# The recurrence's gate projection as seven products, with tokens on partitions

## The chip, the cores and the metric

The kernel runs on one core of a Trainium2 chip. Its time is the device time of one execution in microseconds (us). It uses five engines: TensorE (PE) multiplies matrices, VectorE (DVE) and ScalarE (ACT) work elementwise, GpSimd (POOL) does a little arithmetic and issues slow transfers, SyncE (SP) issues most loads. Each engine runs its own list of instructions in order, and a semaphore makes it wait where it needs another engine's result or a transfer.

## What is computed

One layer on x, 512 tokens by 2048 features, in float32:

```python
h = rms_norm(x, norm_w)
q, k, v, g_attn, xr, g_lru = split(h @ w_in)      # w_in: 2048 x (1024|256|256|1024|1024|1024)
attn_out = attention(q, k, v)                     # 8 heads, 2 key/value heads, q and k normed and roped
lru_out = rg_lru(xr, forward) + rg_lru(xr, backward)
mixed = concat(rms_norm(attn_out) * silu(g_attn), rms_norm(lru_out) * silu(g_lru))
return x + mixed @ w_out                          # w_out: 2048 x 2048
```

The change concerns g_lru, the 1024 columns of w_in that start at C_GL = 3584.

## The kernel before

**Precision.** A float32 operand is held as a pair of rounded tiles, high and low part: x as xh and xl, a weight tile as wh and wl. mm3 makes one product out of three matmuls: high by high, high by low, low by high. A weight tile of 128 x 512 is loaded by SP into wr (three buffers of two tiles), ACT rounds it to wh (wsplit, L219), DVE subtracts to get wl (L221). x is normed by norm_w alone; the factor 1/rms of a token, rstd, is multiplied in when a projection leaves PSUM.

**Two layouts.** proj_feat gives features on partitions and tokens along the row (the weight tile is the stationary operand): four PSUM banks of 128 features x 512 tokens. Its result has to be multiplied by rstd along the row, so rows() turns rstd (128 x 4) by a transpose on PE, copies the line to line_sb on DVE, writes it to DRAM and reads it back broadcast to all partitions as rbc (two transfers on POOL's queue, L295 and L296). evac_bc then multiplies a bank by rbc on DVE (L395) into an ev tile and so frees the bank. proj_tok gives tokens on partitions; evac_tok scales by rstd[:, t] on ACT. PSUM has eight banks: four for projections (pj) and four for the rest (mm).

**Stages.** PE's instructions run in the order of the program, which weaves a projection (fill) with a chain that consumes earlier results: weave() takes from the chain how many units of fill to run next. The stages are:
- C_XR, first half, while x is still being loaded and split; then xstats makes rstd and rbc.
- C_XR + 512 woven with the recurrence of the first half (lru_half(0)); C_K (k and v) with the second (lru_half(1)).
- C_Q and C_Q + 512 woven with kv(). Each q half ends in evac_tok and norm_rope: ACT sums squares (L533), POOL makes the factors (L281, L282), DVE multiplies and ropes (L538 to L547). kv() also makes r_l, the factor 1/rms of the recurrence's output, and its broadcast gbc.
- gates(): C_GL, C_GL + 512 and the first half of C_GA, 96 units of six to twelve matmuls, woven with attention(). attention() first turns q of two heads (turned(): four transposes each, split by ACT L562 and DVE L563 into the pair b), yields 13 units, and then asks for the first scores. In between normed() multiplies hp, the recurrence's output, by gbc, and gate() multiplies by the silu of the gates.
- C_GA + 512 woven with later(), and then the output projection. It is already done as seven products of half size instead of eight (Strassen's scheme in Winograd's form), whose sums of w_out are made in DRAM by transfers that accumulate: sums_in_dram() issues 32 of them on POOL's queue, one for every second unit of gates().

DVE, ACT and SP get their order from a scheduler that sorts by priority and by when operands come. Weight splits stand under high_priority(AHEAD = 600), the attention's softmax under a smaller one. The order of PE and, in the attention's part, of POOL is that of the code.

**Ring.** aring and hring are rings of SBUF from which the late tiles are cut; hp holds the recurrence's output by feature, ap_ the attention's (av).

Of the kernel before, what the change touches and what calls it, by code (L numbers as in the profile page):

```python
# [17 lines left out]
P = 128  # L18
# [13 lines left out]


LRU_K2, LRU_B4 = 12, 9
ATT_K2, ATT_B4, ATT_PT = 9, 4, 2


AHEAD = 600
# [6 lines left out]


SOON = 40


H = 256  # L50
# [9 lines left out]
def hybrid_kernel(  # L60
# [68 lines left out]

    def ev():  # L130

        for pool, n in (("lru", 4), ("qkv", 8), ("fin", 4)):
            if pool in pools:
                return pools[pool].tile([P, SEQ], F32, tag="ev", bufs=n, name=nm("ev"))

# [9 lines left out]
    def f(ap):  # L145
        return ap.bitcast(F32)
# [11 lines left out]
    nhalf = const([P, 48], "nhalf")  # L158
    nc.gpsimd.memset(nhalf, -0.5)

    nw_st = const([KT, P], "nw_st")
    vec_st = const([R_END, P], "vec_st")

    def vec_load():
# [139 lines left out]

    def proj_feat(c0, acc, first=None, given={}):

        acc += [pj() for _ in range(4)]
        for c in range(KT // 2):  # L310
            if c == 0 and first:

                for k, (wh, wl) in enumerate(first):
                    for j, (w, x_) in enumerate(((wh, xh), (wl, xh), (wh, xl))):
                        for e in range(4):
                            nc.tensor.matmul(  # L316
                                acc[e], w[:, e * P : (e + 1) * P], x_[k],
                                start=k == 0 and j == 0, stop=False,
                            )
# [5 lines left out]
            ws = given[c] if c in given else wload(w_in, c * 2 * P, c0)  # L325
            for e in range(4):
                es = slice(e * P, (e + 1) * P)
                for k, (wh, wl) in enumerate(ws):
                    kk = 2 * c + k
                    mm3(acc[e], wh[:, es], wl[:, es], xh[kk], xl[kk], kk == 0, kk == KT - 1)  # L330
                yield c, e

    def tok_block(acc, w, r0, c0, lh, ll, nk):

        acc += [pj() for _ in range(NT)]
        for c in range(nk // 2):
            ws = wload(w, r0 + c * 2 * P, c0)
            for t in range(NT):
# [222 lines left out]
    def split_ps(pt, hi, lo):  # L561
        nc.scalar.copy(hi, pt)  # L562
        nc.vector.tensor_sub(lo, pt, f(hi))  # L563

    def kv(es):
# [15 lines left out]
        r = group_rstd(sums["l"], "r_l", NB * P)  # L581
        yield 4
        rows(gbc, r)

    def turned(rot, h):

# [36 lines left out]
    def values(h, pth, ptl):  # L623

        gs = slice(h // G * HD, (h // G + 1) * HD)
        o = mm()
        for s in range(NT):
            mm3(o, vh[s][:, gs], vl[s][:, gs], pth[:, s, :], ptl[:, s, :], s == 0, s == NT - 1)
        if h % 2 == 0:
            ap_[h // 2] = aring.tile([P, 2, SEQ], F32, name=nm("av"))  # L630
        av, asum = ap_[h // 2][:, h % 2, :], sums["a"]
        nc.vector.tensor_copy(av, o)
        if h == 0:
            nc.scalar.activation(asum, av, AF.Square)
        else:
            sq = k2()
            nc.scalar.activation(sq, av, AF.Square)
            nc.gpsimd.tensor_add(asum, asum, sq)

    def attention(rots):  # L640

        qs, ps_, pts = {h: turned(rots[0], h) for h in range(2)}, {}, {}
        yield 13
        for d in range(2 * NH + 3):
            h, half = divmod(d - 4, 2)
            if h >= 0 and half == 0:
# [128 lines left out]
        for c in range(4)  # L775
    ]

    def sums_in_dram():

        def two(c, k, j):  # L780
            r0 = mixed[2 * c][0]
            w = w_out[r0 : r0 + 4 * P, j * SEQ : (j + 1) * SEQ]
            return w.rearrange("(n k p) e -> p k n e", k=2, p=P)[:, k]

        def put(c, t, src):
            nc.gpsimd.dma_start(tsum[c][t], src)

        def add(c, t, src):
            nc.gpsimd.dma_start(tsum[c][t], src, accum_op=ALU.add)

        for c0 in (0, 2):
            cs = (c0, c0 + 1)
# [4 lines left out]
                yield add(c, TA, two(c, 0, 0))  # L797
                yield add(c, TB, two(c, 0, 0))
            for c in cs:
                yield put(c, TC, tsum[c][TA])  # L800
            for c in cs:
                yield add(c, TC, two(c, 1, 0))
            for c in cs:
                yield put(c, TD, tsum[c][TC])
            for c in cs:
                yield add(c, TD, two(c, 1, 1))

    def out_loads(g, second, i):

# [226 lines left out]

    s1.close()
    lru_consts()
    jobs = sums_in_dram()
    fill = proj_feat(C_XR + SEQ, a2)  # L1040
    weave(fill, lru_half(0, a1))
    drain(fill)
# [20 lines left out]

    def both():
        yield from q_proj(C_Q, a4)
        yield from q_proj(C_Q + SEQ, a5)

    fill = both()
    weave(fill, kv(kvs))
    drain(fill)  # L1070

    closed("rot", "rope", "wx")
    sums["a"] = pools["qkv"].tile([P, SEQ], F32, tag="asum", name="asum")
    opened("att", "right")

    late = []

    def gates():
        todo = iter(())
        for n, (c0, row) in enumerate(((C_GL, R_LN), (C_GL + SEQ, R_LN + 4), (C_GA, R_AN))):  # L1080
            acc, wait = [], 8 * (n > 0)
            for k, _ in enumerate(proj_feat(c0, acc)):
                if 32 * n + k >= 16 and k % 2 == 0:
                    next(jobs, None)
                if n == 0 and k >= 16 and k % 4 == 0:
                    normed(hp[k // 4 - 4])
                if wait == 0:
                    wait = next(todo, 99)
                wait -= 1
                yield  # L1090
            if n < 2:
                todo = gate(evac_bc(acc), hp[2 * n : 2 * n + 2], row, k2)
            else:
                late.extend(evac_bc(acc))

    fill = gates()
    with tc.manual_schedule(engines={mybir.EngineType.Pool}):
        weave(fill, attention(rots))
        for _ in range(6):
            next(fill)  # L1100
    r = group_rstd([sums["a"]], "r_a", NH * HD)
    closed("att", "qkv")
# [17 lines left out]
    def later():  # L1120
        for pair in ap_[:2]:
            normed(pair)
        yield 6
        todo = gate(late, ap_[:2], R_AN, fin_s)
        for _ in range(3):
            yield next(todo)
# [82 lines left out]
```

## Time and profile before

| | us |
|---|---|
| median of 3 runs | 650.33 (650.0 to 650.38) |
| the profiled execution, own time | 650.22 |
| its span | 648.4 |
| PE busy | 643.5 (99%) |
| DVE busy | 476.4 (73%) |
| ACT busy | 347.1 (54%) |
| POOL busy | 94.8 (15%) |

The span is the time from the first to the last instruction in the trace; about 1.8 us of the execution lie around it. PE's busy time counts overlapping matmuls once. The gates run from 255 to about 440 us, the output projection after it.

### The profile page before, as it was taken

The numbers are of one execution on the slowest core, as the hardware profiler recorded it, in microseconds if no ns is written. First come the engines' busy times: TensorE is split into PE (matmuls) and PEld (weight loads), VectorE is DVE, ScalarE is ACT, GpSimd is POOL, SyncE is SP. The second block draws the span as 40 slices with busy tenths as digits, with TensorE's granted clock in tenths as the row PEclk, the third lists the DMA queues.
The fourth block names the chain that finished last, engine by engine and source line by source line (L and its number), as shares of the span: only waits on it lengthen the run. The fifth ranks groups of instructions, "written<-read, shape, count | busy, mean of one in ns | idle before, by whom it ended". The sixth has DMA issues, their size and how long they took to land.

```text
span 648.4 us, 8619 instructions
## 1 busy us (share of the span) xinstructions
PE 643.5 (99%) x2979; PEld 534.0 (82%) x2979; DVE 476.4 (73%) x821; ACT 347.1 (54%) x639; POOL 94.8 (15%) x126
## 2 busy tenths in 40 slices
PE   9999999999999999999999999999999999999997
PEld 6888888888888888888888888888888888888886
DVE  5877679986788935855765566637967978699994
ACT  3543799489856615444474444635444654443441
POOL 0000000000012312123434435311000000010000
PEclk9999999999999999999999999999999999999999
DMA  8943243322234331357676858763354857686322
GB/s 290 304 128 111 66 137 99 92 71 66 83 99 144 98 114 33 109 148 173 117 191 174 204 122 202 184 131 113 98 184 166 324 166 238 202 281 211 120 92 98
DMA packets 53211, 96.96 MB, mean 150 GB/s; under 512 B 4332, under 2 KB 14960, under 8 KB 53040
## 3 DMA queue, kind: packets, MB, share of 16 engines
q1 hardware_dynamic: 45936, 75.56, 36.6%
q0 software_dynamic: 7056, 20.72, 14.2%
q8 instruction: 23, 0.38, 0.2%
q14 instruction: 20, 0.16, 0.1%
q10 hardware_dynamic: 176, 0.14, 0.1%
HBM read 92.21 MB, written 20.98 MB: 175 GB/s over the span
## 4 chain that ended last, share of the span: by engine, by line
PE 99%; DVE 0%; issue 0%
PE pj L150 20%; PE pj L151 20%; PE pj L149 20%; PE mm L944 13%; PE pj L944 11%; PE mm L151 3%; PE mm L149 3%; PE mm L150 3%; PE mm L619 2%; PE mm L251 1%; PE pj L316 1%; PE mm L558 1%; PE mm L983 0%; PE mm L692 0%; DVE xt L927 0%; PE mm L292 0%
## 5 line engine op out<-in xcount | busy, mean ns | idle before, releaser
L149 PE MATMUL pj<-x,wh 128*128 128x512 f32 x376 | 147.6, 392 | 0.0
L151 PE MATMUL pj<-x,wl 128*128 128x512 f32 x376 | 146.5, 390 | 0.0
L150 PE MATMUL pj<-x,wh 128*128 128x512 f32 x376 | 146.5, 390 | 0.0
L219 ACT CAST wh<-wr 128x512 fp32r<-128x512 f32 x143 | 85.0, 619 | 76.4 <-PE pj L151 18.7
L221 DVE TENSOR_TENSOR wl<-wr,wh 128x512 fp32r<-128x512 f32 (+1 forms) x145 | 101.1, 724 | 33.3 <-ACT wh L219 32.7
L150 PEld LDWEIGHTS pj<-x,wh 128*128 128x128 f32 x376 | 70.6, 188 | 14.9 <-DVE x L254 0.4
L151 PEld LDWEIGHTS pj<-x,wl 128*128 128x128 f32 x376 | 70.6, 188 | 14.8
L149 PEld LDWEIGHTS pj<-x,wh 128*128 128x128 f32 x376 | 70.6, 188 | 14.7
L755 ACT CAST oh<-rw 128x512 fp32r<-128x512 f32 x94 | 56.3, 620 | 38.7 <-PE mm L944 15.5
L149 PE MATMUL pj<-wh,x 128*128 128x512 f32 x192 | 75.0, 391 | 0.0
L151 PE MATMUL pj<-wh,x 128*128 128x512 f32 x192 | 74.7, 389 | 0.0
L150 PE MATMUL pj<-wl,x 128*128 128x512 f32 x192 | 74.7, 389 | 0.0
L756 DVE TENSOR_TENSOR ol<-rw,oh 128x512 fp32r<-128x512 f32 x94 | 61.9, 688 | 10.7 <-ACT oh L755 10.4
L944 PE MATMUL mm<-ol,mh 128*128 128x512 f32 (+1 forms) x128 | 49.0, 382 | 0.0
L944 PE MATMUL mm<-oh,ml 128*128 128x512 f32 (+1 forms) x128 | 48.9, 382 | 0.0
L944 PE MATMUL mm<-oh,mh 128*128 128x512 f32 (+1 forms) x128 | 48.9, 382 | 0.0
L149 PEld LDWEIGHTS pj<-wh,x 128*128 128x128 f32 x192 | 36.0, 188 | 7.6
L150 PEld LDWEIGHTS pj<-wl,x 128*128 128x128 f32 x192 | 36.1, 188 | 7.4
L151 PEld LDWEIGHTS pj<-wh,x 128*128 128x128 f32 x192 | 36.0, 188 | 7.4
L944 PE MATMUL pj<-oh,mh 128*128 128x512 f32 (+1 forms) x104 | 39.7, 382 | 0.0
L944 PE MATMUL pj<-ol,mh 128*128 128x512 f32 (+1 forms) x104 | 39.7, 382 | 0.0
L944 PE MATMUL pj<-oh,ml 128*128 128x512 f32 (+1 forms) x104 | 39.6, 381 | 0.0
(209 smaller groups left out, 1062.9 us busy)
## 6 DMA issues: line engine op xcount, KB each, us to landing
wr<-in_w_in_dram SPq DMA_DIRECT2D x71, 512.0 KB, 3.8
rw<-in_w_out_dram SPq DMA_DIRECT2D x63, 256.0 KB, 3.8
ts<-in_w_out_dram POOLq DMA_DIRECT2D x24, 512.0 KB, 6.6
rw<-ts SPq DMA_DIRECT2D x31, 256.0 KB, 4.4
ts<-ts POOLq DMA_DIRECT2D x8, 512.0 KB, 8.0
xt<-in_x_dram SPq DMA_DIRECT2D x8, 512.0 KB, 8.6
b<-in_x_dram SPq DMA_DIRECT2D x7, 512.0 KB, 7.8
out_dram<-xt POOLq DMA_DIRECT2D x12, 256.0 KB, 3.4
```

Of the source, the lines that this page charges most:

```text
L149: nc.tensor.matmul(acc, lh, rh, start=start, stop=False)
L150: nc.tensor.matmul(acc, lh, rl, start=False, stop=False)
L151: nc.tensor.matmul(acc, ll, rh, start=False, stop=stop)
L219: rounded(hi[:, c], raw[:, k, c])
L221: nc.vector.tensor_sub(lo[:, c], raw[:, k, c], f(hi[:, c]))
L251: nc.tensor.transpose(pt[:, t * P : (t + 1) * P], xc[:, h * n + t, ks], ident)
L316: nc.tensor.matmul(acc[e], w[:, e * P : (e + 1) * P], x_[k], start=k == 0 and j == 0, stop=False,)
L558: nc.tensor.transpose(pt[:, t * P : (t + 1) * P], rot[t][:, h, :], ident)
L619: nc.tensor.transpose(pt[:, s * P : (s + 1) * P], p[:, s * P : (s + 1) * P], ident)
L755: nc.scalar.copy(hi, src)
L756: nc.vector.tensor_sub(lo, src, f(hi))
L944: nc.tensor.matmul(bank[key][:, to], lh[:, a, ts_], rh[:, cols], start=i == 0 and j == 0, stop=i == 7 and j == 2,)
```

## The change

It makes C_GL's projection in seven products, each of 256 tokens x 512 columns x 1024 features, on two PSUM banks (gl_units). The products are named P1, Q6, P2, Q5, Q3, Q7, Q4.
- **Weight sums.** Four combinations of w_in's blocks for each of four chunks (gsum) are made in DRAM by 32 accumulating transfers on POOL's queue, by the same sums_in_dram as for w_out. These and w_out's now form one list, jobs["all"]. paced() takes one from the list with each weight load from C_XR + 512 on (two at every fifth): DVE copies one column of the newest wl to a mark, POOL copies the mark, and then POOL issues the transfer. gates() takes one from it for every third unit.
- **Sums of x.** x_sums(i), for i = 0 to 7, makes z = xh + xl for two tiles (DVE, 128 x 512 each), then d, four combinations of 128 x 256 (three DVE subtractions, the first 128 x 512), and POOL stores d (512 KB) in DRAM as dsum (ds in the rows below). d and z have two buffers each. Two of the eight run before C_XR + 512 in the program, six during the second q half. In four of the products they come back as draw, 16 loads of 256 KB, and are split into dh (ACT) and dl (DVE).
- **Combining.** product_done adds or subtracts a product's two banks into ev tiles (14 on DVE, 2 copies on ACT); 10 ev tiles instead of 8.
- **Gates.** They come out with tokens on partitions. lru_gates(j) applies silu with scale rstd and the factor r_l by ACT, turns the tiles back by 8 groups of four transposes on PE, and multiplies into hp on DVE. hp's multiplication by gbc, and r_l's rows(), go.
- **C_GA's first half** runs as two passes of 256 columns (ga_units, G and H) among C_GL's units, in the order of PLAN; the heads 0 and 1 are gated early (heads_gates).
- **Attention** yields 4 units ahead of its first scores instead of 13; av is copied on ACT instead of DVE; the pools k2 and b4 are smaller.

```diff
+    def x_sums(i):
+        z, d = zs[i % 2], ds_[i % 2]
+        for k in range(2):
+            nc.vector.tensor_add(z[:, k, :], f(xh[2 * i + k]), f(xl[2 * i + k]))
+        src, a = halves(z), nc.vector.tensor_tensor
+        a(d[:, 0:2], src[:, 0:1].broadcast_to([P, 2, H]), src[:, 1:3], op=ALU.subtract)
+        a(d[:, 2], src[:, 1], d[:, 1], op=ALU.subtract)
+        a(d[:, 3], src[:, 3], d[:, 2], op=ALU.subtract)
+        nc.gpsimd.dma_start(dsum[i // 2][:, :, i % 2, :], d)
...
     def attention(rots):
         qs, ps_, pts = {h: turned(rots[0], h) for h in range(2)}, {}, {}
-        yield 13
+        yield 4
...
             elif d < 2 * NH + 2:
-                yield sum(STEPS)
+                yield 2
...
+    for i in range(XS_FIRST):
+        x_sums(i)
+    jobs["all"] = itertools.chain(sums_in_dram(gsum, two_gl), sums_in_dram(tsum, two_out))
     fill = proj_feat(C_XR + SEQ, a2)
     weave(fill, lru_half(0, a1))
...
+        for n, _ in enumerate(q_proj(C_Q + SEQ, a5)):
+            if n % 4 == 3 and n // 4 + XS_FIRST < KT // 2:
+                x_sums(n // 4 + XS_FIRST)
+            yield
...
+    def gl_units(banks):
+        nd = 0
+        for name, left, right in PRODUCTS:
+            for c in range(4):
+                with tc.high_priority(AHEAD):
+                    raw = pools["wr"].tile([P, 2, SEQ], F32, tag="wr", bufs=3, name=nm("wr"))
+                    nc.sync.dma_start(
+                        raw, gsum[c][right] if isinstance(right, int) else two_gl(c, *right)
+                    )
+                    if isinstance(left, int):
+                        draw = draws[nd % 2]
...
+                        nc.scalar.copy(dh, draw)
+                        nc.vector.tensor_sub(dl, draw, f(dh))
+                    ws = [wsplit(raw, n) for n in range(2)]
+                for n, (wh, wl) in enumerate(ws):
+                    i = 2 * c + n
+                    for s, bank in enumerate(banks):
...
+                        mm3(bank, lh, ll, wh, wl, i == 0, i == KT // 2 - 1)
+                    if i == KT // 2 - 1:
+                        product_done(name, banks)
+                    yield name if i == KT // 2 - 1 else None
...
+    def lru_gates(j):
+        tiles = [halves_of[n, s] for n in (("c", "d"), ("b", "a"))[j] for s in range(2)]
+        for t, tile_ in enumerate(tiles):
+            nc.scalar.activation(tile_, tile_, AF.Silu, scale=rstd[:, t : t + 1])
+        yield
+        for t, tile_ in enumerate(tiles):
+            nc.scalar.activation(tile_, tile_, AF.Identity, scale=r_lru[0][:, t : t + 1])
+        yield
+        for m in range(4):
+            pt = mm()
+            for t, tile_ in enumerate(tiles):
+                nc.tensor.transpose(
+                    pt[:, t * P : (t + 1) * P], tile_[:, m * P : (m + 1) * P], ident
+                )
...
+    PLAN = "uuuuG" "uuuuG" "uuuuG" "uuGuuG" "uuGuuG" "uuuuG" "uuuu" "HHHHHHHH"
```

The order moves at two seams. The first is the end of C_XR's first half. POOL's list there, before, has rstd, then the line and the broadcast rbc, and then the factors of k:

```order
L281 TENSOR_SCALAR rstd<-xsum 128x4
L282 TENSOR_TENSOR rstd<-rstd,nhalf 128x4
L295 DMA line_601<-line_sb 4x128
L296 DMA rbc<-line_601 128x512
L281 TENSOR_SCALAR rr_1683<-rr_1683 128x2
```

Now, with ds the stores of d_719 and d_720 (the two buffers of d), L285 and L286 the former L281 and L282, and L299 and L300 the former L295 and L296:

```order
L848 DMA ds_141<-d_719 512x1x256
L285 TENSOR_SCALAR rstd<-xsum 128x4
L286 TENSOR_TENSOR rstd<-rstd,nhalf 128x4
L848 DMA ds_141<-d_720 512x1x256
L299 DMA line_629<-line_sb 4x128
L300 DMA rbc<-line_629 128x512
L321 COPY mark_91<-mark_91 128x1
L817 DMA gs_125<-in_w_in_dram 256x1x512
```

One store stands ahead of rstd and one between rstd and the line. DVE's list up to line_sb's copy at the same place, before, holds the constants of the recurrence (lc):

```order
L371 RECIPROCAL lc_659<-lc_659 128x16
L372 TENSOR_TENSOR lc_659<-lc_659,lc_658 128x16
L373 TENSOR_TENSOR lc_660<-lc_659 128x16
L374 TENSOR_SCALAR lc_661<-lc_660 128x16
L376 TENSOR_TENSOR lc_661<-lc_661,lc_660 128x16
L377 TENSOR_SCALAR lc_661<-lc_661 128x16
L293 COPY line_sb<-mm_598 4x128
```

Now L843 is a sum z, and L845, L846 and L847 are the three subtractions of d:

```order
L225 TENSOR_TENSOR wl_653<-wr_650,wh_652 128x512
L225 TENSOR_TENSOR wl_657<-wr_650,wh_656 128x512
L189 COPY vec<-mm_591 128x104
L845 TENSOR_TENSOR d_720<-z_718 128x512
L386 TENSOR_SCALAR lc_685<-vec 128x16
L843 TENSOR_TENSOR z_717<-x_92_385,x_93_386 128x512
L387 TENSOR_TENSOR lc_685<-lc_685,vec 128x16
L846 TENSOR_TENSOR d_720<-z_718,d_720 128x256
L297 COPY line_sb<-mm_626 4x128
```

The copy to line_sb stands behind the subtraction that writes d_720 anew, which needs the store of d_720 to have ended.

The second seam is the start of the gates. PE's list ahead of the first scores, before (b_509 is the pair of head 0's q, kt_2208 the keys; pj_2522 to pj_2525 are the banks of C_GL, thirteen units after the transposes of q):

```order
L150 MATMUL pj_2522<-x_62_313,wh_2630 128x512
L151 MATMUL pj_2522<-x_61_312,wl_2631 128x512
L149 MATMUL pj_2522<-x_64_321,wh_2634 128x512
L150 MATMUL pj_2522<-x_65_322,wh_2634 128x512
L151 MATMUL pj_2522<-x_64_321,wl_2635 128x512
L149 MATMUL mm_2644<-kt_2208,b_509_2506 128x512
L150 MATMUL mm_2644<-kt_2208,b_509_2506 128x512
L151 MATMUL mm_2644<-kt_2208,b_509_2506 128x512
```

Now (b_533_2705 is the same pair, and pj_2721 and pj_2722 are the first product's banks, four units after the transposes):

```order
L152 MATMUL pj_2721<-wh_2754,x_82_340 128x512
L153 MATMUL pj_2721<-wl_2755,x_82_340 128x512
L154 MATMUL pj_2721<-wh_2754,x_83_341 128x512
L152 MATMUL pj_2722<-wh_2754,x_82_340 128x512
L153 MATMUL pj_2722<-wl_2755,x_82_340 128x512
L154 MATMUL pj_2722<-wh_2754,x_83_341 128x512
L152 MATMUL mm_2771<-kt_2365,b_533_2705 128x512
L153 MATMUL mm_2771<-kt_2365,b_533_2705 128x512
L154 MATMUL mm_2771<-kt_2365,b_533_2705 128x512
```

There are 24 matmuls between the transposes and the scores instead of 78. DVE's list there, before, ends the rope work of the second q half (sq_2491 and ev_2427 are its last tile) and then splits q of heads 0 and 1 (L563):

```order
L538 TENSOR_TENSOR ev_2427<-ev_2427,rr_2462 128x512
L540 TENSOR_TENSOR sq_2491<-ev_2427,rq 128x8x32 x2
L546 TENSOR_TENSOR ev_2427<-ev_2427,rq 128x512
L547 TENSOR_TENSOR ev_2427<-ev_2427,sq_2491 128x512
L221 TENSOR_TENSOR wl_2631<-wr_2628,wh_2630 128x512
L563 TENSOR_TENSOR b_509_2506<-mm_2507,b_509_2506 128x512
L221 TENSOR_TENSOR wl_2635<-wr_2628,wh_2634 128x512
L563 TENSOR_TENSOR b_511_2514<-mm_2515,b_511_2514 128x512
```

Now, with L582 the split of q, dl the low parts of the reloaded sums of x, and mx the first row maximum of the scores:

```order
L557 TENSOR_TENSOR ev_2623<-ev_2623,rr_2658 128x512
L565 TENSOR_TENSOR ev_2621<-ev_2621,rq 128x512
L559 TENSOR_TENSOR sq_2687<-ev_2623,rq 128x8x32
L566 TENSOR_TENSOR ev_2621<-ev_2621,sq_2681 128x512
L559 TENSOR_TENSOR sq_2687<-ev_2623,rq 128x8x32
L565 TENSOR_TENSOR ev_2623<-ev_2623,rq 128x512
L566 TENSOR_TENSOR ev_2623<-ev_2623,sq_2687 128x512
L1180 TENSOR_TENSOR dl_2895<-draw_2701,dh_2894 128x512
L1180 TENSOR_TENSOR dl_2949<-draw_2702,dh_2948 128x512
L582 TENSOR_TENSOR b_533_2705<-mm_2706,b_533_2705 128x512
L582 TENSOR_TENSOR b_535_2713<-mm_2714,b_535_2713 128x512
L626 TENSOR_REDUCE mx_2775<-mm_2771 128x1
```

The split of q stands behind all of the rope work still, and behind two low parts that were not there before.

More of the change, by code (lines that the diff above doesn't have):

```diff
@@ L303, in xstats, with paced @@
         rows(rbc, rstd)
+    jobs, job_of = {}, [0]
+    def paced(ws):
+        if "all" in jobs:
+            wl = ws[1][1]
+            for _ in range(2 if job_of[0] % 5 == 3 else 1):
+                m = marks[job_of[0] % len(marks)]
+                job_of[0] += 1
+                nc.vector.tensor_copy(m[:, 0:1], f(wl[:, 0:1]))
+                nc.gpsimd.tensor_copy(m[:, 8:9], m[:, 0:1])
+                next(jobs["all"], None)
     def proj_feat(c0, acc, first=None, given={}):
@@ L580, in kv @@
             split_ps(turn(rot, h), kth[h], ktl[h])
-        r = group_rstd(sums["l"], "r_l", NB * P)
-        yield 4
-        rows(gbc, r)
+        r_lru.append(group_rstd(sums["l"], "r_l", NB * P))
     def turned(rot, h):
@@ L1079, in gates @@
         todo = iter(())
[L1080 to L1092, printed above, removed]
-            else:
-                late.extend(evac_bc(acc))
+        for n, unit in enumerate(itertools.chain.from_iterable((u, u) for u in PLAN)):
+            done = next(units[unit])
+            if n % 3 == 0:
+                next(jobs["all"], None)
+            if done == "Q4":
+                todo = itertools.chain(todo, lru_gates(1))
+            elif unit == "G" and len(early) == 2 and n == PLAN.rindex("G") * 2 + 1:
+                todo = itertools.chain(lru_gates(0), heads_gates(early))
+            else:
+                next(todo, None)
+            yield
@@ L1123, in later @@
         yield 6
-        todo = gate(late, ap_[:2], R_AN, fin_s)
-        for _ in range(3):
-            yield next(todo)
+        todo = gate(late, ap_[1:2], R_AN + 2, fin_s)
+        yield next(todo)
         drain(
```

130 lines of the change are left out of this document (113 added, 17 removed).

## The prediction

> **What bounds the kernel now.** I read first the busy time and the waits, then the chain that ended last. These rows are the page's line of busy times, its row of the granted TensorE clock, the one row of the view of waits that belongs to PE, and the head of the chain.
>
> ```profile
> PE 643.5 (99%) x2979; PEld 534.0 (82%) x2979; DVE 476.4 (73%) x821; ACT 347.1 (54%) x639; POOL 94.8 (15%) x126
> PEclk9999999999999999999999999999999999999999
> PE mm L983 <- DVE ones L156: 1.0, 1, 1.0
> PE 99%; DVE 0%; issue 0%
> ```
>
> PE works 643.5 of 648.4 us, the chain is PE from end to end, and PE's only wait on another engine in the whole run is 1.0 us at the very start. So two questions decide: how much PE work the change removes, and whether PE, which never waits today, begins to wait. Every microsecond of either goes into the end whole. DVE (73%) and ACT (54%) matter only where PE comes to wait for them. Next I read the timeline of PE, for the price of a matmul and of a group of transposes.
>
> ```profile
> 53.72 0.39 PE L150 MATMUL pj<-x,wh 128*128 128x512 f32 x1
> ...
> 56.89 0.39 PE L149 MATMUL pj<-x,wh 128*128 128x512 f32 x1
> ...
> 58.48 0.39 PE L150 MATMUL pj<-x,wh 128*128 128x512 f32 x1
> ...
> 296.02 0.60 PE L558 MATMUL mm<-ident,ev 128*128 128x128 f32 x4
> 296.37 0.48 PE L149 MATMUL mm<-kt,b 128*128 128x512 f32 x1
> 296.69 0.40 PE L150 MATMUL mm<-kt,b 128*128 128x512 f32 x1
> ```
>
> A record lasts 0.39 us, but the records overlap. From 53.72 to 58.48 lie 21 steps, so a matmul costs 4.76/21 = 0.2267 us. Four transposes hold the next matmul off by 0.35 (296.02 to 296.37), and that matmul is followed after 0.32 instead of 0.23, so a group of four costs about 0.44.
>
> **The matmuls.** C_GL's 1024 columns took 2 x 16 x 4 x 3 = 384 matmuls; seven products of 8 k-tiles x 2 banks x 3 are 336. Removed: 48 x 0.2267 = 10.9 us. The gates now come out with tokens on partitions, and 8 groups of four transposes turn them: 8 x 0.44 = 3.5. One transposed row fewer (r_l) is below my rounding. C_GA's first half in two passes of 256 columns keeps its count. PE's own work falls by 7.4 us.
>
> **Start of C_XR+512 (first seam).** The four banks of C_XR are freed by evac_bc, which multiplies by rbc, the broadcast of rstd. These are the steps to rbc in the timelines of DVE and POOL, in order of time, and below them DVE's load in two stretches.
>
> ```profile
> 43.21 0.19 DVE L300 TENSOR_REDUCE xsum<-ssq 128x4 f32<-128x32 f32 x1
> 43.49 0.56 POOL L281 TENSOR_SCALAR rstd<-xsum 128x4 f32<-128x4 f32 x1 [42.17 <-DVE xsum L300]
> 44.13 1.04 POOL L282 TENSOR_TENSOR rstd<-rstd,nhalf 128x4 f32<-128x4 f32 x1
> 49.12 0.27 DVE L293 COPY line_sb<-mm 4x128 f32<-4x128 f32 x1
> 51.80 0.60 POOL L296 DMA_DIRECT2D rbc<-line  x1 [1.35 <-DMA line<-line_sb]
> 55.64 1.89 DVE L395 TENSOR_TENSOR ev<-pj,rbc 128x512 f32<-128x512 f32 x3 [2.18 <-DMA rbc<-line]
> 20.00:40.00 20.00, 20.00 (x108) 16.95 (x107) 16.43 (x52) 10.40 (x18) 0.00 (x0) 1.00 0.80 269
> 40.00:60.00 20.00, 20.00 (x90) 16.39 (x90) 15.25 (x53) 5.37 (x10) 2.92 (x4) 1.00 0.40 119
> ```
>
> line_sb to the first eviction takes 6.5 us, the bank is free at 55.64 + 1.89/3 = 56.3, and PE takes it at 56.89: slack 0.6. In the new order three things come ahead. DVE gets some twenty x_sums operations (0.69 us each) among C_XR's, where it is already busy 16.43 and 15.25 of 20 us; by a walk along its rows xsum comes near 45.4 instead of 43.2, and rstd near 47.4. Then POOL issues the transfer ds of the second d right after rstd, and on DVE line_sb's copy now stands behind the subtraction that overwrites that d, so behind the landing. No 512 KB store like it is in this trace. The nearest rows of the DMA issues:
>
> ```profile
> out_dram<-xt POOLq DMA_DIRECT2D x12, 256.0 KB, 3.4
> ts<-in_w_out_dram POOLq DMA_DIRECT2D x24, 512.0 KB, 6.6
> ts<-ts POOLq DMA_DIRECT2D x8, 512.0 KB, 8.0
> ```
>
> The first has the direction with half the bytes, the second the bytes; I take 5, with 3.4 and 8.0 as ends. After landing, the waiting subtraction, one sum, one half-wide subtraction and two small constants run ahead of the copy, about 2.2 us: 47.4 + 5 + 2.2 = 54.6. Six and a half later, plus 0.7 for the eviction, gives 61.8 for the bank, against a demand of 57.5 (0.6 later than before, since one z stands ahead of an early xl on whose heels PE runs). Stall 4.3, and with that 0.6: **+4.9**, ends 3.3 and 7.9. If the scheduler's sums were covered after all it would be 0. The lc constants and wh casts behind line_sb have their cover in the same wait.
>
> **Start of the gates and of attention (second seam).** The last q chunk ends, eight transposes turn q of heads 0 and 1, and attention yields 13 gate units before its first scores; now it yields 4. The timelines of PE, ACT and DVE there, and the load of the engines:
>
> ```profile
> 254.56 0.39 PE L151 MATMUL pj<-wh,x 128*128 128x512 f32 x1
> 254.78 1.03 PE L558 MATMUL mm<-ident,ev 128*128 128x128 f32 x8
> 255.57 0.48 PE L149 MATMUL pj<-x,wh 128*128 128x512 f32 x1
> ...
> 273.36 0.39 PE L149 MATMUL mm<-kt,b 128*128 128x512 f32 x1
> ...
> 266.37 0.58 ACT L562 CAST b<-mm 128x512 fp32r<-128x512 f32 x1
> ...
> 255.26 0.69 DVE L538 TENSOR_TENSOR ev<-ev,rr 128x512 f32<-128x512 f32 x1 [5.05 <-POOL rr L282]
> ...
> 267.76 0.69 DVE L547 TENSOR_TENSOR ev<-ev,sq 128x512 f32<-128x512 f32 x1
> 268.37 0.68 DVE L221 TENSOR_TENSOR wl<-wr,wh 128x512 fp32r<-128x512 f32 x1
> 268.98 0.68 DVE L563 TENSOR_TENSOR b<-mm,b 128x512 fp32r<-128x512 f32 x1
> ...
> 255.00:260.00 5.00, 5.00 (x28) 4.24 (x27) 4.31 (x8) 4.62 (x22) 2.94 (x5) 1.00 0.03 5
> 260.00:265.00 5.00, 5.00 (x24) 4.14 (x23) 4.97 (x11) 1.65 (x6) 2.62 (x3) 1.00 0.32 101
> 265.00:270.00 5.00, 5.00 (x24) 4.14 (x23) 4.90 (x10) 2.21 (x4) 0.00 (x0) 1.00 0.37 108
> ```
>
> The low part of q (L563) is finished at 268.98 + 0.68 = 269.7, 14.9 us after the q chunk's end at 254.78, because DVE first does the norm and rope of the second half of q (255.26 to 268.4, and full: 4.97 and 4.90 of 5). PE asked for it at 273.8, so there were 4.1 us of slack. In the new order the split (now L582) still stands behind all of that rope work, which can't start earlier, since it waits for the last q chunk. Before it stand one weight low part more and two low parts of d: 3 x 0.69 = 2.1. So the split is ready 14.9 to 17.0 after the chunk's end. PE asks 0.8 (transposes) + 24 x 0.2267 = 5.4 + two score matmuls 0.45 = 6.7 after it. Stall 8.2 to 10.3; I take **+10.0**, near the upper end, as DVE had almost no gap to take the three in. ACT's high part (266.37 before) is no later than DVE's.
>
> **The gates stage.** It lasts 160 us; these rows are its load, then the groups by which I price what is added.
>
> ```profile
> 270.00:430.00 160.00, 160.00 (x784) 134.01 (x783) 96.03 (x165) 81.75 (x160) 58.87 (x70) 1.00 0.69 165
> L221 DVE TENSOR_TENSOR wl<-wr,wh 128x512 fp32r<-128x512 f32 (+1 forms) x145 | 101.1, 724 | 33.3 <-ACT wh L219 32.7
> L219 ACT CAST wh<-wr 128x512 fp32r<-128x512 f32 x143 | 85.0, 619 | 76.4 <-PE pj L151 18.7
> L704 DVE TENSOR_TENSOR hs<-hs,gbc 128x1024 f32<-128x1024 f32 x4 | 4.7, 1223 | 2.8 <-DMA gbc<-line 2.8
> ```
>
> Weight tiles to split grow from 32 to 56, and 16 draws come: DVE gains 40 x 0.72 and 14 combines of about 0.69, and loses 8 evictions and 8 copies of av (0.69) and the four products with gbc (1.22): 96.0 + 28.8 + 9.7 - 11.0 - 4.9 = 118.6 of about 152 us (78%). ACT gains 40 x 0.62, ten copies and eight scalings of 0.7: 81.8 + 24.8 + 12.6 = 119 (78%). Both keep room; I found no row where PE must wait, and each product's two banks are free again within the 4 to 7 us that other units cover. I cost it at nothing, ends 0 and +3. Loads grow by 12 weight loads of 512 KB and 16 draws of 256 KB, 10 MB on the 26.4 MB that 165 GB/s moved here, while eight of the pacing jobs have gone ahead into earlier stages, where the DMA share was .40 and less. Cost 0; if the loads came late, the same +3 holds it. The marks on DVE and POOL, the remaining x_sums beside the q projection (DVE rows wait there for ds transfers, 5 to 15 us ahead of need by my walk) and the forty weight jobs delay nothing that PE asks for: 0, end +1.
>
> **Sum**, against the profiled execution's 650.2 (the median of the runs shown is 650.33, the span 648.4): 650.2 - 10.9 + 3.5 + 4.9 + 10.0 = **657.7**.
>
> **A rule of the skill.** No stretch of this trace shows the clock below 1.00, and none shows PE idle in mid-run. The Trainium skill, "TensorE: Matmul & The Clock Gate", section "Part 1: The HAM clock gate", says that the array falls to half clock after an idle window of about 3.4 us and needs as long a busy one to come back; no run here shows it yet. By it, half of 3.4 us would be lost after each seam, an estimate of 1.7 to 3.4 each, and the sum would be 661 to 664.
>
> **Rivals.**
> - Only the second seam binds. POOL's store lands early or DVE has more room in C_XR than I walked: 650.2 - 7.4 + 10.0 = 652.8. For it: seam one rests on durations that the trace doesn't have. Against: slack there is only 0.6.
> - The other side: the split of q isn't late. If DVE reached it within 6.7 us of the chunk's end (that is, if the two heads' splits ran ahead of the rope work), the seam would cost 0, and with the first seam's 4.9 the time would be 650.2 - 7.4 + 4.9 = 647.7; without that too, 642.8. It decides when both seams together cost under 6.1 us. For it: the work needed is only two operations of 0.69. Against: the order of the DVE rows is fixed and puts them last.
> - PE runs slow after its waits. With starts 0.453 apart instead of 0.2267 for 8 to 15 matmuls after each stall, 1.7 to 3.4 are lost twice: 661 to 664. For it: stalls of this length are new. Against: no row.
> - The gates stage starves as well: with both engines at 78%, a wait of 0.5 at half of the seven product changes and of the eight transposing groups adds 3 to 4: 661.
>
> **How the numbers follow.** Both seams 0.48; only the second 0.20; the other side 0.14; slow clock or starving stage 0.12; in between, seam costs that cancel the saving, 0.06. A measurement of this kernel can tell 0.2%, 1.3 us, from no change. Faster 0.15, same 0.07, slower 0.78. The likeliest case alone spans 654 to 661. The range reaches to the second-seam case and part of the other side below, and over the slow clock's lower end above: 648 to 663.
>
> **What would show it.** Right: PE's waits hold one before C_XR+512's first matmul at 57 to 62, released by DVE's eviction, which itself waits for rbc; and one of 8 to 10 before the scores near 262, released by DVE L582; PE's count of records falls by about 17. After the stalls the granted clock tells the third rival. Wrong: if PE's waits stay near 1.0, if the score matmul follows at once, or if the wait at 60 is absent.

## The result and the profile after

The changed kernel takes 727.34 us (median of 4 runs, 726.16 to 730.25) against 650.28: ratio 1.1192, 95% interval 1.1159 to 1.1226. That is 77 us slower, where 7.5 were forecast. These lines of the page after answer to those of before: busy times, granted clock, head of the chain.

```profile
PE 651.6 (90%) x2962; PEld 535.2 (74%) x2962; DVE 515.7 (71%) x944; ACT 380.4 (52%) x699; POOL 154.1 (21%) x214
PEclk9999999999999787855899999999999999999999
PE 58%; issue 13%; DVE 11%; ACT 7%; DMA 6%; POOL 5%; SPq 0%; DVEq 0%; POOLq 0%; ACTq 0%
```

The span grew from 648.4 to 726.0, and PE is idle for 726.0 - 651.6 = 74.4 us of it instead of 4.9. The waits of PE, in the columns total, number, longest:

```profile
PE pj L153 <- DVE wl L225: 54.0, 5, 27.4
PE mm L152 <- ACT b L581: 7.6, 1, 7.6
PE pj L152 <- ACT ev L540: 2.6, 1, 2.6
PE pj L152 <- DVE ev L414: 1.7, 1, 1.7
PE pj L152 <- DVE mark L320: 1.5, 1, 1.5
```

The two seams of the prediction are here: 7.6 (and 0.7 for the low part) at the first scores, 1.7 ahead of C_XR+512. The 54.0 us are not in the prediction; 53.0 of them lie between 244 and 331, in four waits: 11.1 and 10.9 in the second q half, 3.6 and 27.4 in the first units of the gates right behind it. Three rows of the view of all waits, and one of the same view of the kernel before, say who stands behind DVE:

```profile
DVE ev L557 <- POOL rr L286: 50.2, 3, 28.6
DVE d L845 <- DMA ds<-d: 21.5, 3, 8.4
POOL gs L820 <- issue: 39.7, 9, 7.5
```

```profile
POOL ts L789 <- issue: 33.5, 9, 7.4
```

DVE waits 50.2 us for rr, the norm factors of q, which POOL makes, and 21.5 for the stores of d, which POOL issues. By DVE's timeline PE's waits of 11.1 and 27.4 (38.4 together) stand behind rr, those of 10.9 and 3.6 (14.5) behind the stores. POOL itself stands up to 7.5 us ahead of an accumulating transfer (L820), with nothing that the profile shows to wait for. The kernel before had that wait too, 33.5 us in nine places, at the same instruction under its old line number, during the attention, where nothing asked for POOL soon. The longest case, in POOL's timeline, then the rows of DVE and PE that it releases:

```profile
307.17 0.80 POOL L848 DMA_DIRECT2D ds<-d  x1 [7.06 <-issue]
...
310.68 1.07 POOL L820 DMA_DIRECT2D ts<-in_w_out_dram  x1 [2.52 <-issue]
311.27 0.67 POOL L321 COPY mark<-mark 128x1 f32<-128x1 f32 x1
317.23 1.05 POOL L820 DMA_DIRECT2D ts<-in_w_out_dram  x1 [5.29 <-issue]
...
323.77 1.05 POOL L820 DMA_DIRECT2D ts<-in_w_out_dram  x1 [5.30 <-issue]
324.35 1.52 POOL L817 DMA_DIRECT2D ts<-ts  x2
325.94 0.19 POOL L285 TENSOR_SCALAR rr<-rr 128x4 f32<-128x4 f32 x1
```

```profile
327.29 0.69 DVE L557 TENSOR_TENSOR ev<-ev,rr 128x512 f32<-128x512 f32 x1 [28.61 <-POOL rr L286]
...
330.14 0.69 DVE L225 TENSOR_TENSOR wl<-wr,wh 128x512 fp32r<-128x512 f32 x1
330.89 0.79 PE L153 MATMUL pj<-wl,x 128*128 128x512 f32 x1 [27.36 <-DVE wl L225]
```

The second q half had left PE by 293, and the sums of squares for its factors were there by 296. POOL's list has seven more transfers ahead of the factors, four of them accumulating, which follow each other at 6.5 us. The wait stands ahead of the next transfer and not behind the last: the copy of a mark right behind an accumulating transfer ran at once (311.27), and so did the first factor behind the last transfers (325.94). DVE waits 28.6 us with the first rope product, and the next weight's low part stands behind it; PE waits 27.4 for that low part.

The 77.6 us of span add up. By the gaps in PE's timeline, waits in mid-run are 69.4. The matmuls between them are slower: 49 start 0.43 after the one before instead of 0.227 (9.8 us), the first after each wait is late by 0.2 (2.7), other irregular steps cost 4.0 more than before. The stretches of transposes and warm-up cost 2.7 more, and 48 matmuls fewer save 10.9: 69.4 + 9.8 + 2.7 + 4.0 + 2.7 - 10.9 = 77.7.

### The profile page after: what moved, and what is told of

Its sections match the earlier page's. It is cut to its first block, busy times and chain, and to the rows that moved or that the text cites. A ratio compares the mean times of both kernels' runs of the same rounds, so it can differ in the third digit from the quotient of the medians.

```text
span 726.0 us, 9022 instructions
## 1 busy us (share of the span) xinstructions
PE 651.6 (90%) x2962; PEld 535.2 (74%) x2962; DVE 515.7 (71%) x944; ACT 380.4 (52%) x699; POOL 154.1 (21%) x214
## 4 chain that ended last, share of the span: by engine, by line
PE 58%; issue 13%; DVE 11%; ACT 7%; DMA 6%; POOL 5%; SPq 0%; DVEq 0%; POOLq 0%; ACTq 0%
PE mm L986 12%; PE pj L986 9%; PE pj L152 9%; PE pj L153 9%; PE pj L154 9%; DVE wl L225 3%; PE mm L154 2%; PE mm L152 2%; PE mm L153 2%; DMA wr<-in_w_in_dram 2%; DVE b L498 2%; PE mm L638 2%; ACT wh L223 1%; DMA k<-in_lru_wx_dram 1%; POOL rr L286 1%
## 5 line engine op out<-in xcount | busy, mean ns | idle before, releaser
L153 PE MATMUL pj<-wl,x 128*128 128x512 f32 x240 | 98.6, 411 | 54.0 <-DVE wl L225 54.0
L152 PE MATMUL pj<-wh,x 128*128 128x512 f32 x240 | 98.4, 410 | 4.1 <-ACT ev L540 2.6
L152 PE MATMUL pj<-x,wh 128*128 128x512 f32 x248 | 98.0, 395 | 2.0 <-DVE ev L414 1.7
L154 PE MATMUL pj<-wh,x 128*128 128x512 f32 x240 | 97.7, 407 | 0.0
L153 PE MATMUL pj<-x,wh 128*128 128x512 f32 x248 | 96.7, 390 | 0.8 <-DVE x L258 0.8
L154 PE MATMUL pj<-x,wl 128*128 128x512 f32 x248 | 96.8, 390 | 0.0
L153 PEld LDWEIGHTS pj<-wl,x 128*128 128x128 f32 x240 | 47.8, 199 | 66.0 <-DVE wl L225 56.0
L152 PEld LDWEIGHTS pj<-wh,x 128*128 128x128 f32 x240 | 47.5, 198 | 15.2 <-ACT ev L540 3.0
L152 PEld LDWEIGHTS pj<-x,wh 128*128 128x128 f32 x248 | 46.6, 188 | 12.3 <-issue 2.1
L154 PEld LDWEIGHTS pj<-wh,x 128*128 128x128 f32 x240 | 47.7, 199 | 10.4
L153 PEld LDWEIGHTS pj<-x,wh 128*128 128x128 f32 x248 | 46.6, 188 | 10.6 <-DVE x L258 1.2
L154 PEld LDWEIGHTS pj<-x,wl 128*128 128x128 f32 x248 | 46.5, 188 | 10.2 <-DVE wl L225 0.4
L321 POOL COPY mark<-mark 128x1 f32<-128x1 f32 x50 | 31.3, 644 | 97.6 <-DVE mark L320 97.6
L631 POOL TENSOR_SCALAR k<-k,sm 128x512 f32<-128x512 f32 x32 | 27.8, 880 | 79.5 <-DVE sm L630 61.5
L557 DVE TENSOR_TENSOR ev<-ev,rr 128x512 f32<-128x512 f32 x8 | 5.5, 686 | 50.2 <-POOL rr L286 50.2
```

Of the source, the lines that this page charges most:

```text
L152: nc.tensor.matmul(acc, lh, rh, start=start, stop=False)
L153: nc.tensor.matmul(acc, lh, rl, start=False, stop=False)
L154: nc.tensor.matmul(acc, ll, rh, start=False, stop=stop)
L321: nc.gpsimd.tensor_copy(m[:, 8:9], m[:, 0:1])
L631: nc.gpsimd.tensor_scalar(p, p, sm, 0.0, op0=ALU.mult, op1=ALU.add)
```

## The experiments

Times of each are medians of two to five runs beside runs of the kernel before (650.2 to 650.4). The variants differ by up to 1.1% from run to run, the kernel before by 0.3%; differences under 5 us between the variants are therefore read from the traces and not from the times.

### The jobs alone, added to the kernel before

```diff
+    jobs["all"] = itertools.chain(sums_in_dram(True), sums_in_dram(False))   # C_GL's sums, then w_out's
     fill = proj_feat(C_XR + SEQ, a2)
...
             ws = wload(w, r0 + c * 2 * P, c0)
+            paced(ws)
```

> The kernel before, with only the paced weight sums added: the marks, C_GL's 32 jobs and the first 8 of w_out's, paced over the weight loads of C_XR+512, C_K and q, POOL in the order of the code there. No seven products, no sums of x, no stores of d; nobody reads C_GL's sums. Theory A: the jobs alone hold POOL ahead of q's factors: PE waits of 35 to 55 us in the q projections, time 690 to 710. Rival C (the stores of d are needed for it): 650 to 658. Rival B (bytes): waits on wr by ACT, spread over all stages, 655 to 670.

Measured 696.72 us, ratio 1.0713 (1.0626 to 1.0801). From the views of waits, all and PE's:

```profile
DVE ev L554 <- POOL rr L282: 37.7, 3, 21.7
PE mm L292 <- POOL r_l L282: 14.1, 1, 14.1
PE pj L150 <- DVE wl L221: 12.6, 2, 12.2
PE pj L151 <- DVE wl L221: 6.8, 1, 6.8
```

No product, no sum of x and no store of d is needed: the 40 paced transfers alone cost 46 us, by POOL's factors (rr, and here r_l, for which PE waits directly). In the profiled run 36 us of it are PE's waits; the rest includes 27 matmuls at half speed behind them.

### The jobs moved out of the q projections

```diff
-            for _ in range(2 if job_of[0] % 5 == 3 else 1):
+            for _ in range(per_load[0]):          # 2 in C_XR+512 and C_K, 0 in the q projections
...
-            if n % 3 == 0:
+            if n % 5 in (0, 2):
                 next(jobs["all"], None)
```

> The changed kernel with two jobs for every weight load of C_XR+512 and C_K, none during the two q projections, and w_out's 32 jobs all in the gates (two of every five units instead of one of three). Theory A: no job stands ahead of q's factors, so PE's waits of 53 us between 235 and 345 fall below 10; but POOL has 32 jobs in some 135 us, 16 accumulating at 6.5 and 8 copies at about 5, so the factors of k may come 10 to 20 us late: 660 to 680. Rival B (bytes): the same traffic in less time, so over 700. Rival C (stores of d, which no longer queue behind jobs): as A, but with DVE's waits for ds gone and those for rr left.

Measured 666.73 us, ratio 1.0252 (1.0222 to 1.0282): 60.6 us less than the changed kernel, with the same transfers. PE's four longest waits:

```profile
PE mm L152 <- ACT b L581: 8.1, 1, 8.1
PE mm L255 <- DMA b<-in_x_dram: 2.1, 1, 2.1
PE pj L152 <- DVE ev L414: 1.7, 1, 1.7
PE pj L152 <- DVE mark L320: 1.5, 1, 1.5
```

The four waits of 53.0 us are gone. The transfers and their bytes are the same in all, so it is not their amount but where they stand in POOL's list that cost them.

### Transfers without accumulation

```diff
-            nc.gpsimd.dma_start(sum_[c][t], src, accum_op=ALU.add)
+            nc.gpsimd.dma_start(sum_[c][t], src, **({} if pacing[0] else {"accum_op": ALU.add}))
```

> The changed kernel, but the jobs that are issued ahead of the gates write without accumulating: same number of transfers at the same places of POOL's list, same marks, same bytes written, the old content not read (what they leave in DRAM are no sums). Theory A (an accumulating transfer holds POOL until the one before it has landed, some 6.5 us each, and the factors rr of q, which POOL makes, stand behind it; DVE waits for rr, PE for the wl behind): DVE's wait for rr falls from 50.2 to under 10 us, PE's waits from 70 to some 15, time about 660 (655 to 668). Rival B (the extra bytes make the weight loads late, ACT's wait for wr of 32.2 us): bytes fall by little, so over 690. Rival C (DVE waits for the stores of d and for the marks): unchanged by this edit, so over 690.

Measured 689.45 us, ratio 1.0601 (1.0569 to 1.0634): 38 us less than the changed kernel, but 29 more than theory A said. POOL's rows for the same four jobs, first the changed kernel's second to fourth, then this one's:

```profile
213.21 1.05 POOL L820 DMA_DIRECT2D gs<-in_w_in_dram  x1 [4.44 <-issue]
219.84 1.05 POOL L820 DMA_DIRECT2D gs<-in_w_in_dram  x1 [5.39 <-issue]
226.41 1.04 POOL L820 DMA_DIRECT2D gs<-in_w_in_dram  x1 [5.33 <-issue]
```

```profile
210.19 0.65 POOL L820 DMA_DIRECT2D gs<-in_w_in_dram  x1
211.59 0.65 POOL L820 DMA_DIRECT2D gs<-in_w_in_dram  x1
214.54 0.65 POOL L820 DMA_DIRECT2D gs<-in_w_in_dram  x1 [2.10 <-issue]
```

Accumulating ones follow each other at 6.6 us; plain ones go out at 0.9 to 3. DVE's wait for rr falls from 50.2 to 26.6. So the long hold belongs to accumulation, but theory A was too narrow: a plain transfer holds POOL as well when others are under way (2 to 5.6 us in this run), a copy of one sum into the next waits for the landing, and DVE still waits 18.8 us in this run for stores of d in the same queue.

### The second seam alone

The kernel before with `yield 4` for `yield 13`.

> The kernel before with one number changed: attention yields 4 units instead of 13 ahead of its first scores. By the prediction's second seam the split of q is ready 14.9 us after the q chunk's end and PE asks for it 0.8 + 5.4 (24 matmuls) + 0.45 after it, less what the units of this kernel are longer or shorter: a wait of 8.2 (7 to 9), time 658.4. With a half clock for 3 to 4 us after the wait, as the changed kernel shows after each wait over 2.5 us: 1.7 to 2.2 more, 660.3. Rival (the wait is made up later, or the units differ): 650 to 652.

Measured 663.7 and 669.4 us, ratio 1.025 (1.0146 to 1.0354). PE's two waits, and POOL's row ahead of the second:

```profile
PE mm L151 <- DVE b L563: 6.1, 1, 6.1
PE mm L292 <- POOL r_a L282: 2.9, 1, 2.9
443.85 1.06 POOL L789 DMA_DIRECT2D ts<-in_w_out_dram  x1 [6.99 <-issue]
```

With 1.0 for the high part the seam costs 7.1, near the 8.2 expected, and 12 matmuls at half speed behind it 2.4. The rest was not expected: the attention ends nine units sooner, and r_a, made by POOL, now meets an accumulating transfer. These rows are of the run of 663.7; what made the other one 5.7 longer no trace shows.

### What the split of q waits for

In the kernel with the early jobs, ACT's row of that split names the releaser; L565 is the rope product that reads the table last:

```profile
279.35 1.07 ACT L581 CAST b<-mm 128x512 fp32r<-128x512 f32 x2 [1.42 <-DVE ev L565]
```

```diff
-        q = b4(F32R)
-        soon(split_ps, turn(rot, h), q[:, 0, :], q[:, 1, :])
+        if h >= 2:
...
+        else:
+            q = pools["qkv"].tile([P, 2, SEQ], F32R, tag="q01", bufs=2, name=nm("q01"))
+            pt = turn(rot, h)
+            with tc.high_priority(AHEAD):
+                split_ps(pt, q[:, 0, :], q[:, 1, :])
```

> On top of e3_jobs_early: the pairs of q of heads 0 and 1 get tiles of their own in the pool that is open since kv(), instead of tiles that reuse the space of the rope tables, and their split stands under the high priority; for the space, the marks have 2 columns instead of 16 and the attention's two pools 5 and 2 buffers instead of 7 and 3. In e3 PE waited 8.1 + 0.7 us for ACT's and DVE's split, and ACT's split waited for the last reader of the rope table. Theory A (the wait at the start of the attention is a matter of that space, not of DVE's load): the split now runs behind the first of four tiles of rope work, PE's wait falls to under 1, the half clock after it (11 matmuls, 2.4 us) goes too: 666.7 - 8.8 - 2.4 = 655.5 (653 to 657). Rival (DVE simply has too much to do there: the wait moves to the weights' low parts behind): 662 to 667.

Measured 662.46 us (660.1 to 667.4), about 4 less by the medians. Its best run, 660.1, is still above the 657 expected at most. The wait for the split is gone; in DVE's timeline it comes right behind the first of the four tiles:

```profile
273.23 0.69 DVE L566 TENSOR_TENSOR ev<-ev,sq 128x512 f32<-128x512 f32 x1
273.85 1.28 DVE L582 TENSOR_TENSOR q<-mm,q 128x512 fp32r<-128x512 f32 x2
```

PE waits instead 2.9 us at a later score, for the softmax on ACT, with 6 matmuls at half speed, and smaller ones follow. So both are true: the split was late because its space was the rope table's, and once it isn't, ACT and DVE are late elsewhere there. The edit changes the space and the priority of the split together; that it is the space rests on ACT's row above, and the two were not run apart.

### The small steps in between

All eight sums of x in the second q half (XS_FIRST = 0), then one mark for each load, then another division of the attention's buffers:

> e6_own_q with all eight x_sums in the second q half (XS_FIRST 0 instead of 2), so that no store of d stands between rstd and rbc on POOL. The wait ahead of C_XR+512's first matmul (1.7 us in the changed kernel and in e3) goes, as far as the store caused it: 1.5 to 2 us less than e6, 653.5. Rival (the six more stores and sums make the q projection wait): 656 to 665.

> e7_own_q_xs0 with one mark for each weight load, followed by two jobs, instead of a mark for each job, so that DVE meets POOL half as often; marks of 16 columns again. In e3 PE waited 1.5 and 1.1 us for DVE work that stood behind marks, and a mark waits until POOL has read the mark eight places earlier. Theory A: these 2.6 us go, 651 (649.5 to 652.5); with nothing left but the work on PE, 650.2 - 7.4 = 643 is the floor. Rival (POOL can't do two jobs for each load, whatever the marks): no change from e7.

> e8_one_mark with the attention's pools at 7 and 1 buffers instead of 5 and 2. If the softmax has too few buffers in e8, this is 1 to 5 us faster than e8; if the pairs of q have, as much slower; else the same within 0.5.

Measured 668.43 (664.3 to 670.9), 667.19 (662.7 to 669.9) and 667.97 (664.3 to 670.6): by their times they are not clearly apart from the one before, and the first two did not bring the 653.5 and 651 that were expected. In the traces, the first does what it should: the wait of 2.2 us ahead of C_XR+512 goes. One mark takes away the wait of 1.5; ACT's weight cast, late by 2.4 us before, is late by 3.5 in the one kernel with one mark and by 1.7 in the other. The buffers make no difference in time.

In these kernels, and in the one with early jobs, C_XR itself had become slow: rbc's first use was at 60.7 to 63.2 us, in the kernel before at 55.64. That was the experiments' own doing. Two of w_out's jobs that depend on nothing had been put at the very start of POOL's list.

```diff
-            if n % 5 in (0, 2):
+            if n >= 12 and n % 2 == 0:
                 next(jobs["all"], None)
```

> e7_own_q_xs0, but the gates issue w_out's jobs from their 13th unit on, every second unit. In e3 and e6 to e9 the first two jobs of the gates depend on nothing and stand at the very start of POOL's list; C_XR's matmuls ended near 62 there instead of 57, with waits for x in the first 11 us. If these two transfers beside the loads of x are the reason, the stage ends near 57 again and the time falls by 4 to 5 us against e7 (668.4): 663.5 (660 to 666). Rival (x_sums and z make DVE late there): no change.

Measured 663.28 us (661.1 to 665.7), 5 less than the 668.43 of its base, and rbc's first use is at 56.23, where its base had 60.87. Two transfers of 512 KB beside the loads of x cost that stage 4.6 us. This version and the one of 662.46 have the lowest medians with the whole computation, and both are 2% slower than the kernel before.

### A few jobs back in the q projections, and a later start of the attention

The base is the kernel just told, of 663.28 us. One job for every two loads comes back into the q projections, eight in all.

```diff
-            for _ in range(per_load[0]):
+            nload[0] += 1
+            for _ in range(per_load[0] - nload[0] % 2):   # 1.5 early, 0.5 in the q projections
```

> e10_jobs_not_first with three jobs for every two weight loads of C_XR+512 and C_K and one for every two of the q projections, instead of two for each and none. Theory A: in the early stages POOL keeps up (1.5 jobs for each 10 us), so the waits at 111 (ACT's wh, 2.4), 120 and 142 (marks, 2.6) go; in q at most one transfer of 6.5 us stands ahead of the factors, which are wanted at the end of each half: a wait of 0 to 6 there. 659 (656 to 664). Rival (any job ahead of q's factors costs its whole 6.5 twice): 670 and more.

Measured 672.13 us, 9 us more than its base, as the rival said. The early waits came to about the same in all, and around the q projections the wait came back:

```profile
PE pj L153 <- DVE wl L225: 14.0, 2, 11.3
```

With twenty, eight and no jobs in that stage PE waits about 56, 14 and under 2 us there. The longest wait, 11.3 us, is longer than the 6.5 of one accumulating transfer: stores of d stand in the same list between the jobs, and in this run DVE waits 12.0 us for them and 18.0 for rr.

With eight units ahead of the first scores instead of four:

> e11_three_of_two with 8 units instead of 4 ahead of the first scores (three units fewer behind the attention). In e7 and e9 PE waited 2.9 to 4.2 us at the scores of the first heads for the softmax on ACT, which shares ACT with the squares of q's norm. With four units, 5.4 us, later, that wait and its half clock go: 3 to 5 us less than e11. Rival (the wait moves with the scores): same as e11, or slower by the cover missing at the end.

Measured 672.16, the same: the wait of 1.8 us for the softmax at the first heads went, but a wait of 12.0 behind the q projections stayed, a later one of 2.4 in the attention stayed as 2.6, and the second product then waited 1.3 for the split sums of x.

### The change without its weight sums

The base is the kernel just told. It leaves out the weight sums: no jobs ahead of the gates, and four products load a plain block of w_in of the same shape.

> e12_yield8 without the weight sums: no jobs and no marks ahead of the gates, and the products that need a sum load a block of w_in of the same shape instead. All else of the change is there (seven products, sums of x and their stores, transposes). What is left should be the change's gain on PE without its transfers: 650.2 - 7.4 = 642.8, plus waits of the start of the attention and of the q projection for the stores of d, 0 to 6: 645. If it stays over 655, the sums of x or the load of the gates cost as much as the weight sums.

Measured 652.14 us, ratio 1.0047 (1.0024 to 1.0071). The page's line of busy times, PE's longer waits, and the load of the gates' stretch:

```profile
PE 637.6 (98%) x2962; PEld 527.5 (81%) x2962; DVE 517.0 (80%) x894; ACT 380.1 (58%) x699; POOL 106.4 (16%) x132
PE mm L152 <- DVE pt L584: 2.0, 2, 1.8
PE pj L154 <- DVE dl L1189: 1.6, 1, 1.6
270.00:430.00 160.00, 154.45 (x760) 127.87 (x759) 121.92 (x206) 113.53 (x217) 61.73 (x69) 1.00 0.84 219
```

PE's work does fall, by 5.9 us instead of the 7.4 worked out. But waits of 7.6 us take it back, 1.7 of them in the first 15 us and the rest in the gates: DVE and ACT, at 76% and 71% of that stretch, are late by up to 1.8 us in a handful of places. Even with free weight sums, the one version run here does not beat the kernel before.

## Why the prediction was wrong

- **The term that failed** is this: "the forty weight jobs delay nothing that PE asks for: 0, end +1". It measured 53.0 us of PE's waits from the second q half to the first units of the gates (and the half clock behind them), 38.4 behind q's factors and 14.5 behind the stores of d. DVE's waits for the stores, put in the same sentence at 5 to 15 us ahead of need, were 21.5 us, and the stores were late behind the jobs in POOL's list. The prediction gave no reason for the jobs' zero: it walked POOL's order at the first seam only, and never asked what stands behind a job. The price stood in the profile of before: POOL's wait of 33.5 us ahead of nine accumulating transfers, and their 6.6 us to landing. In the changed kernel POOL issued six accumulating transfers and four copies from 206 to 248 us, 42 us, where a whole q half takes 192 matmuls of 0.2267 us, 43.5. The factors of the first q half stood behind them in the list: its last bank was read at 222, and its factors came from 249 on.
- **The matmuls and transposes**: -7.4 forecast, -5.9 where nothing else disturbs. Right in kind; the first matmul after each wait costs 0.2 more.
- **The first seam**: +4.9 forecast, measured 1.7 ahead of C_XR+512 and 0.8 for the low part of x (at 13.6 us). Of the mechanism, DVE's sums ahead of line_sb's copy were right. The wait for the landing of the store, taken at 5 us, is not in the trace: the subtraction that rewrites d starts right behind the instruction before it, and DVE has no gap there. The copy came at 51.93 where 54.6 was forecast. The rows, and the row of the stores in the transfers of the changed kernel:

```profile
46.41 0.75 POOL L848 DMA_DIRECT2D ds<-d  x1
50.06 0.26 DVE L189 COPY vec<-mm 128x104 f32<-128x104 f32 x1
50.23 0.68 DVE L845 TENSOR_TENSOR d<-z 128x512 f32<-128x512 f32 x1
...
51.93 0.27 DVE L297 COPY line_sb<-mm 4x128 f32<-4x128 f32 x1
ds<-d POOLq DMA_DIRECT2D x8, 512.0 KB, 3.6
```

- **The second seam**: +10.0 forecast, 8.3 measured, 7.1 alone. Its place in the order and its size held; it came at 341 us and not near 262, since all before it was late. The reason given, DVE's order, was one of two: the tile's space was tied to the rope table. So the wait ended with ACT's high part (L581), which the prediction took to be no later than DVE's, and not with L582.
- **The gates**: 0 forecast, with ends 0 and +3. In the changed kernel this held, but it looks like luck: PE had just waited 8.3 us at the first scores. With the early jobs, where that wait is 8.8, only 0.2 followed. In the kernels without that wait about 4 to 6 us of waits follow in the gates, and without the weight sums about 6.
- **The rival of the slow clock** was right beside the others: half speed followed all six waits over 2 us in the changed kernel, from the first evictions of q to the first scores. The Trainium skill, "TensorE: Matmul & The Clock Gate", section "Part 1: The HAM clock gate", gives an idle window of about 3.4 us as the condition. Here the measurement differs, and decides: waits of 1.7 to 3.0 us were enough in about half of the cases. By the half of 3.4 us for each wait, an estimate from that page, 1.7 us would be lost. The traces show 1.0 to 2.6 (5 to 13 matmuls at 0.2 more, a slow stretch of 2 to 5.6 us).
- None of the rivals was the one that decided. The range's upper end, 663, came from the seams and the clock, since the jobs had been given an end of +1.

## What to carry to other kernels

An operation that is moved to an idle engine is not free there: look at what else is in that engine's list at that place and who waits for it. POOL was busy 15% before the change and 21% after, and still set the end, since it runs in order and after an accumulating transfer of 512 KB its next transfer went out 6.5 us later. Before adding transfers to a queue, sum these holds over the stage and compare with the stage's length; a small value that others wait for is safe ahead of the transfers, or behind a single one, and not behind a row of them. A wait "issue" at an engine with nothing behind it costs nothing today and is the price of everything that is put behind it tomorrow. And 7 us of saved PE work in a kernel where PE waits nowhere is only worth having when each new operand arrives early; a handful of waits of a microsecond gave it back.

## What the runs showed of the hardware

The half clock after a wait, in PE's timeline and in the granted clock of two windows of the changed kernel (the column after POOL's busy time):

```profile
218.53 0.50 PE L152 MATMUL pj<-wh,x 128*128 128x512 f32 x1 [2.59 <-ACT ev L540]
...
219.10 0.39 PE L154 MATMUL pj<-wh,x 128*128 128x512 f32 x1
...
220.12 0.63 PE L154 MATMUL pj<-wh,x 128*128 128x512 f32 x1
220.55 0.63 PE L152 MATMUL pj<-wh,x 128*128 128x512 f32 x1
...
223.20 0.39 PE L153 MATMUL pj<-wl,x 128*128 128x512 f32 x1
220.00:221.00 1.00, 1.00 (x4) 0.71 (x4) 0.00 (x0) 0.97 (x5) 1.00 (x2) 0.50 0.16 61
223.00:224.00 1.00, 1.00 (x6) 0.83 (x5) 0.07 (x1) 0.94 (x6) 0.00 (x0) 1.00 1.04 184
```

Here the first matmuls after the wait still run at full speed; half speed begins about 1 us later and lasts 3 us. Behind the waits over 4 us that ended in a matmul of this size the first was slow already (0.77 to 0.80 us). Over all runs, no wait under 1.7 us had it, save those of 0.7 right behind one of 7.6 or 8.1. Of waits between 1.7 and 3.0 us some had it (1.7, 1.8, 2.2, 2.4, 2.6 and others, with 5 to 8 matmuls) and some had not (1.7, 1.8, 2.1, 2.4, 2.5 and 2.9), and all over 3.4 us had it (5 to 13 matmuls, 3 where the next wait came first). Whether a wait of about 2 us sets it off can't be told from its length, and a longer wait does not cost a longer slow stretch.
